# Gate, second half: the block sums of pair 10 are given the room of two kept activation sums of down and are fetched right behind the pair's raw tile

## The chip, the cores and the metric

The kernel runs on one core of a Trainium2 chip. What is compared is the time on the device in microseconds (us) for one launch: three runs of the kernel before took 1110.24, 1110.93 and 1111.15 us, and their median, 1110.93 us, stands for it. Beside the runs there is one profiled execution, whose trace names every instruction of the five engines: PE (matrix products; its weight loads are listed apart as PEld), DVE (vector), ACT (scalar), POOL and SP. SP computes nothing here; it issues the DMA transfers one behind the other, and if one has to wait, all behind it wait too. Times inside the execution are counted from the start of its span.

## What is computed

One encoder layer over 256 tokens of width 2048 in float32: a mixer (SSD heads beside pooling heads), a gated conv-MLP, and last a gate for an embedding that belongs to the layer. The change sits in the last of these:

```python
ff = conv_glu(hn, w_ffn_up[i], ffn_conv_w[i], ffn_conv_b[i], w_ffn_down[i])   # ends with "down": 5632 -> 2048
h = h + rmsnorm(ff, ffn_norm_post[i])
gate = jax.nn.sigmoid(rmsnorm(h, ple_norm_pre[i]) @ w_ple_gate[i])            # "gate": 2048 -> 2048
h = h + rmsnorm(gate * (p[i] @ w_ple[i]), ple_norm_post[i])
```

## The kernel before

The stages follow each other: input projection, mixer, output projection, up, down (names that begin with dn), the embedding product (ple) and gate (names that begin with gt). Every large product is made on PE. A weight is split in two parts that PE takes, a rounded one (h, an ACT cast, line 153) and the rest (l, a DVE subtraction, line 154), and each product of two blocks is three matmuls: high by high, low by high, high by low.

Down and gate make their 2048 output columns in two halves of 1024. Each half runs over the input rows in **pairs** of 128-row tiles. A pair is worked in one of two ways:

- plainly: one raw tile of weights (128x2048, 1 MB) is fetched, split in two casts and two subtractions, and gives 24 matmuls of 512 columns;
- with seven products (`seven_products`): the pair and the two groups of 128 tokens make a 2x2 by 2x2 block product, which is done with seven block products instead of eight, on sums of blocks: 21 matmuls. The weights' side of it needs three raw blocks (tile `r`, 128x1536, 768 KB) and four sums of blocks (tile `t`, 128x2048, 1 MB). The split parts are a and b (of r) and d and c (of t). The sums of most pairs were made in the idle time of up and stored in device memory; then `t` is fetched like `r`.

In the second half of gate the pairs come in the order 0, 8, 10, 12, 2, 4, 6, 14 (each named by its first tile), and 8, 10 and 12 are worked with seven products: tiles gt18r, gt18t, gt110r, gt110t, gt112r and gt112t. Behind the last of them, and behind the matmuls of pair 2 (casts gth, rests gtl, raw gt1r), DVE folds the seven products into the four accumulators (`combine`, lines 310 to 324); the matmuls of pair 4 that add to an accumulator come only when its fold is done. Three raw tiles follow pair 12: those of pairs 4, 6 and 14.

**Rooms.** Raw tiles share three rooms, casts and rests five each, and everything of 128x2048 that comes and goes (pages) shares 13 rooms. A tile gets a room when the last reader of the tile before it in that room is done. A fetch is therefore held until its room is free. `seven_products` asks for `t` as a page. In down, three of the activations' sums (k = 8, 18, 24, the list `OWN`) are made once in the first half and kept for the second, each in a room of its own of 128x1024 (`own_place`).

**Order.** In this part of the program no order is written out by hand: a scheduler places the instructions of each engine by when it thinks their operands and rooms are there. A fetch through `load` may be placed freely (`ahead`) or is tied behind the fetch before it (`last["dma"]`); only names that begin with dn1 (`IN_ORDER`) are tied.

Of the kernel before, what the change touches and what calls it, by code (L numbers as in the profile page):

```python
# [11 lines left out]
F32 = mybir.dt.float32  # L12
F32R = mybir.dt.float32r
# [4 lines left out]
P = 128  # L18
# [35 lines left out]
def build(nc, a, out):  # L54
# [6 lines left out]
    with tile.TileContext(nc) as tc, \  # L61
# [9 lines left out]
        def ins(r):  # L71
            return getattr(r, "ins", r)

        def page(name, dtype=F32):
            return gp.tile([P, 2048], dtype, tag="pg", bufs=13, name=name)
# [13 lines left out]
        def mm(o, lhsT, rhs, start, stop):  # L89
            last["pe"] = ins(nc.tensor.matmul(o, lhsT, rhs, start=start, stop=stop, skip_group_check=True))  # L90
# [24 lines left out]
        last, sums_ = {}, {}  # L115

        def load(dst, src, ahead=False):

            with tc.issue_after(last["dma"]) if last and not ahead else nullcontext():
                return ins(nc.sync.dma_start(dst, src))  # L120
# [21 lines left out]
        def split(name, src, nel, cuts=()):  # L142

            if name in ready:
                return ready.pop(name)
            if name in spare:
                hi, lo = spare.pop(name)
            else:
                hi = wp.tile([P, 1056], F32R, tag="whi", bufs=5, name=f"{name}h")
                lo = wp.tile([P, 1056], F32R, tag="wlo", bufs=5, name=f"{name}l")  # L150
            for c0, c1 in zip((0, *cuts), (*cuts, nel)):
                s = slice(c0, c1)
                last["act"] = ins(nc.scalar.copy(hi[:, s], src[:, s]))
                last["dve"] = ins(nc.vector.tensor_sub(lo[:, s], src[:, s], hi[:, s].bitcast(F32)))
            return hi, lo

        def raw(name, src=None):
            r = wp.tile([P, 2048], F32, tag="raw", bufs=3, name=name)
            if src is not None:
                last["dma"] = load(r, src, not name.startswith(IN_ORDER))  # L160
            return r
# [33 lines left out]
        IN_ORDER = ('dn1',)  # L195
# [70 lines left out]
        def add_blocks(r, t=None):  # L266

            v = r.rearrange("p (b c) -> p b c", b=4)
            s = v if t is None else t.rearrange("p (b c) -> p b c", b=4)
            for i, a, b in ((1, v, 0), (0, v, 3), (3, s, 1), (2, s, 3)):  # L270
                nc.vector.tensor_add(s[:, i], v[:, i], a[:, b])  # L271

        def seven_products(name, stage, w, k0, c0, a_, acc, alt, start, stop):

            if (stage, c0, k0) in sums_:
                r = raw(f"{name}r")
                last["dma"] = load(r[:, 512:], w[c0 // 1024, k0 // 2][:, 512:], not name.startswith(IN_ORDER))
                t, held = sums_[stage, c0, k0]  # L280
                if not held:
                    t = page(f"{name}t")
                    last["dma"] = load(t, sums_[stage, c0, k0][0], not name.startswith(IN_ORDER))
            else:
                r = t = raw(f"{name}r", w[c0 // 1024, k0 // 2])
                if stage in APART:
                    t = page(f"{name}t")
                    add_blocks(r, t)
            b11 = split(f"{name}a", r[:, 512:1024], 512)
            b2 = split(f"{name}b", r[:, 1024:], 1024)  # L290
            if r is t:
                add_blocks(r)
            t42 = split(f"{name}d", t[:, 1024:], 1024)
            t31 = split(f"{name}c", t[:, :1024], 1024)

            for x, (wh, wl), c, o, own in (
                    ("a11", b11, 0, alt[0], True), ("a12", b2, 0, acc[0][0], False), ("a22", t42, 0, acc[1][0], False),
                    ("s4", b2, 512, acc[0][1], False), ("s2", t42, 512, alt[3], True), ("s1", t31, 512, alt[1], True),
                    ("s3", t31, 0, alt[2], True)):
                xh, xl = a_[x]  # L300
                for q, (xx, ww) in enumerate(((xh, wh), (xh, wl), (xl, wh))):
                    mm(o, xx, ww[:, c:c + 512], own and start and q == 0, own and stop and q == 2)
# [23 lines left out]
        def token_major(name, w, c0, ks, get, acc, tail=1, fast=(), alt=None, sums=None, at=()):  # L326
# [3 lines left out]
            for u in range(nu):  # L330
# [3 lines left out]
                if u in fast:  # L334
                    if u == fast[0]:
                        alt = alt + [misc(f"{name}s{i}") for i in (2, 3)]
                    seven_products(f"{name}{k0}", name[:2], w, k0, c0, sums(k0), acc, alt, u == fast[0], u == fast[-1])
                    continue
# [143 lines left out]
        for u in range(0, NK, 2):  # L482
            r = [wp.tile([P, 2048], F32, tag="raw", bufs=3, name=f"dtur{u}") if u else r0, page(f"dtur{u + 1}")]
            for j in range(2):
                k = u + j
# [17 lines left out]
            for j in range(2):  # L503
                k = u + j
# [412 lines left out]
        lp = early.enter_context(tc.tile_pool(name="late", bufs=1))  # L917
# [49 lines left out]
        for i, w_ in enumerate(which[2:] + which[:2]):  # L967
            fetch, add, store = block_sums(*w_, i >= len(which) - 2)
            n = 45 * i // 10 + 4
# [135 lines left out]
        own, own_pages = {}, []  # L1105

        def own_place(k):
            n = OWN.index(k)
            if n < 3:
                return lp.tile([P, 1024], F32R, name=f"hd{k}")  # L1110
            if n % 2 == 1:
                own_pages.append(page(f"hd{k}", F32R))
            return own_pages[-1][:, (n - 1) % 2 * 1024:((n - 1) % 2 + 1) * 1024]

        def hid_sums(k):

            (h2, l2), (h1, l1) = get_hid(k, 3 * P), get_hid(k + 1)
            if k in own:
                d = own[k]
            else:  # L1120
                o = own_place(k) if k in OWN else mid(f"hd{k}", F32R)
                if k in kept:
                    nc.gpsimd.dma_start(o.bitcast(F32), kept[k])
                    d = sums_in(o)
                else:
                    d = hid_sums_of(k, sp.tile([P, 512], F32, tag="junk", bufs=1, name=f"hs{k}"), o)
                if k in OWN:
                    own[k] = d
            return dict(d, a11=(h1[:, :P], l1[:, :P]), a12=(h2[:, :P], l2[:, :P]), a22=(h2[:, P:], l2[:, P:]))
# [198 lines left out]
```

## Time and profile before

| | |
|---|---|
| median of three runs | 1110.93 us |
| profiled execution, its own time | 1110.88 us |
| its span | 1109.1 us |
| PE busy | 1099.8 us (99% of the span) |
| DVE busy | 972.4 us (88%) |
| ACT busy | 728.4 us (66%) |
| granted clock of PE, mean | 0.998 |
| transferred over the DMA engines | 362.24 MB, mean 327 GB/s |

Lines of the trace give the start in us, the duration in us, the engine, the line of the kernel and the operation, then the tile written and the tiles read, without buffer numbers (gt110t is one tile; `gt` stands for any of the accumulators of gate), sizes, and the count of merged instructions (x2). In brackets stands how long the engine had been idle before and what ended it. A matmul of 512 columns is listed with some 0.39 us, and in a run without gaps the next begins 0.23 us after it: they overlap, so a late matmul is seen by the distance of two starts.

### The profile page before, as it was taken

The numbers are of one execution on the slowest core, as the hardware profiler recorded it, in microseconds if no ns is written. First come the engines' busy times: TensorE is split into PE (matmuls) and PEld (weight loads), VectorE is DVE, ScalarE is ACT, GpSimd is POOL, SyncE is SP. The second block draws the span as 40 slices with busy tenths as digits, with TensorE's granted clock in tenths as the row PEclk, the third lists the DMA queues.
The fourth block names the chain that finished last, engine by engine and source line by source line (L and its number), as shares of the span: only waits on it lengthen the run. The fifth ranks groups of instructions, "written<-read, shape, count | busy, mean of one in ns | idle before, by whom it ended". The sixth has DMA issues, their size and how long they took to land.

```text
span 1109.1 us, 16105 instructions
## 1 busy us (share of the span) xinstructions
PE 1099.8 (99%) x5949; PEld 948.4 (86%) x5949; DVE 972.4 (88%) x1359; ACT 728.4 (66%) x1065; POOL 74.3 (7%) x146
## 2 busy tenths in 40 slices
PE   9999999999999999999999999999999999999997
PEld 9999988888888888888888888888888888888876
DVE  6589997898879898888888888988999998999996
ACT  7958763556775565655655646657678777877673
POOL 0200000100100000000000000000000000001001
PEclk9999999999999999999999999999999999999999
DMA  9985358556499999999999998999999889996772
GB/s 364 363 334 190 111 192 343 209 217 230 181 358 400 400 399 356 379 362 361 394 358 381 360 388 345 402 358 422 381 393 375 352 332 384 419 388 242 270 294 76
DMA packets 57247, 362.24 MB, mean 327 GB/s; under 512 B 6352, under 2 KB 7248, under 8 KB 21200
## 3 DMA queue, kind: packets, MB, share of 16 engines
q1 hardware_dynamic: 45504, 298.71, 68.9%
q0 software_dynamic: 11232, 61.87, 14.6%
q8 instruction: 47, 0.77, 0.3%
q10 hardware_dynamic: 432, 0.62, 0.2%
q14 instruction: 32, 0.26, 0.1%
HBM read 307.18 MB, written 54.00 MB: 326 GB/s over the span
## 4 chain that ended last, share of the span: by engine, by line
PE 95%; DVE 2%; ACT 1%; issue 1%; DMA 1%; POOL 0%; POOLq 0%; ACTq 0%
PE ga L90 22%; PE va L90 22%; PE dna L90 11%; PE woa L90 6%; PE xbc L90 5%; PE dns L90 4%; PE dtu L90 4%; PE z L90 4%; PE gt L90 4%; PE dn0s L90 2%; PE dn1s L90 2%; PE ple L90 1%; DMA gt112t<-gts 1%; PE yd L90 1%; PE wos L90 1%
## 5 line engine op out<-in xcount | busy, mean ns | idle before, releaser
L90 PE MATMUL ga<-wox,ug_0h 128*128 128x512 f32 x352 | 125.5, 395 | 0.0
L90 PE MATMUL ga<-wox,ug_1h 128*128 128x512 f32 x352 | 125.2, 394 | 0.0
L90 PE MATMUL va<-wox,uv_0h 128*128 128x512 f32 x352 | 124.8, 393 | 0.0
L90 PE MATMUL va<-wox,uv_1h 128*128 128x512 f32 x352 | 124.8, 393 | 0.0
L90 PE MATMUL ga<-wox,ug_1l 128*128 128x256 f32 x352 | 99.1, 282 | 0.0
L90 PE MATMUL va<-wox,uv_0l 128*128 128x256 f32 x352 | 99.1, 281 | 0.0
L90 PE MATMUL va<-wox,uv_1l 128*128 128x256 f32 x352 | 99.1, 281 | 0.0
L90 PE MATMUL ga<-wox,ug_0l 128*128 128x256 f32 x352 | 99.0, 281 | 0.0
L271 DVE TENSOR_TENSOR dnb<-dnb 128x512 f32<-128x512 f32 x128 | 88.3, 690 | 3.0
L90 PEld LDWEIGHTS va<-wox,uv_0h 128*128 128x128 f32 x352 | 66.1, 188 | 15.0
L90 PEld LDWEIGHTS ga<-wox,ug_1h 128*128 128x128 f32 x352 | 66.1, 188 | 15.0
L90 PEld LDWEIGHTS va<-wox,uv_1h 128*128 128x128 f32 x352 | 66.1, 188 | 15.0
L90 PEld LDWEIGHTS ga<-wox,ug_0h 128*128 128x128 f32 x352 | 66.1, 188 | 14.8
L90 PEld LDWEIGHTS ga<-wox,ug_0l 128*128 128x128 f32 x352 | 66.2, 188 | 0.1
L90 PEld LDWEIGHTS ga<-wox,ug_1l 128*128 128x128 f32 x352 | 66.2, 188 | 0.0
L90 PEld LDWEIGHTS va<-wox,uv_1l 128*128 128x128 f32 x352 | 66.2, 188 | 0.0
L90 PEld LDWEIGHTS va<-wox,uv_0l 128*128 128x128 f32 x352 | 66.2, 188 | 0.0
L246 POOL DMA_DIRECT2D dns<-dnb x30 | 16.1, 536 | 320.9 <-DVE dnb L271 280.5
L839 ACT CAST he<-he 128x512 fp32r<-128x512 f32 x13 | 8.1, 620 | 41.1 <-DVE he L838 41.1
L981 ACT CAST hs<-hid 128x384 fp32r<-128x384 f32 (+1 forms) x44 | 23.4, 539 | 16.6 <-PE dna L90 16.3
L1041 ACT ACTIVATE fc<-gr,vt 128x256 f32<-128x256 f32 x44 | 26.1, 594 | 5.9 <-DVE gr L1034 5.9
L398 ACT COPY hid<-va 128x256 f32<-128x256 f32 x44 | 15.6, 372 | 19.5 <-PE va L90 19.5
(2452 smaller groups left out, 3275.5 us busy)
## 6 DMA issues: line engine op xcount, KB each, us to landing
dnb<-w_down SPq DMA_DIRECT2D x32, 1024.0 KB, 9.9
dns<-dnb POOLq DMA_DIRECT2D x30, 1024.0 KB, 5.9
hd<-hsum POOLq DMA_DIRECT2D x25, 512.0 KB, 8.1
zr<-w_z SPq DMA_DIRECT2D x8, 1024.0 KB, 4.8
dtur<-w_dtu SPq DMA_DIRECT2D x14, 528.0 KB, 8.8
hsum<-he POOLq DMA_DIRECT2D x13, 512.0 KB, 8.1
wo0r<-w_out_ SPq DMA_DIRECT2D x6, 1024.0 KB, 7.0
gtb<-w_gate SPq DMA_DIRECT2D x6, 1024.0 KB, 9.5
```

Source lines behind the costliest of these rows:

```text
L90: last["pe"] = ins(nc.tensor.matmul(o, lhsT, rhs, start=start, stop=stop, skip_group_check=True))
L246: nc.gpsimd.dma_start(t, pg[0])
L271: nc.vector.tensor_add(s[:, i], v[:, i], a[:, b])
L398: nc.scalar.copy(o[:, f * L:(f + 1) * L], acc[f][:, L:])
L839: nc.scalar.copy(o[:, :512], s[:, :512])
L981: nc.scalar.copy(t[:, :c1], hid_part(k)[:, :c1])
L1041: nc.scalar.activation(c[:, f], v[:, f], AF.Identity, bias=vec(V_FCB + 4 * s + 2 * i + f), scale=vec(w + NF))
```

## The change

```diff
                 if not held:
-                    t = page(f"{name}t")
-                    last["dma"] = load(t, sums_[stage, c0, k0][0], not name.startswith(IN_ORDER))
+                    t = lp.tile([P, 2048], F32, tag="own", bufs=1, name=f"{name}t") if name == "gt110" else page(f"{name}t")
+                    last["dma"] = load(t, sums_[stage, c0, k0][0], not name.startswith((*IN_ORDER, "gt110")))
...
             if n < 3:
-                return lp.tile([P, 1024], F32R, name=f"hd{k}")
+                if n == 2:
+                    return lp.tile([P, 1024], F32R, name=f"hd{k}")
+                if n == 0:
+                    own_pages.append(lp.tile([P, 2048], F32R, tag="own", bufs=1, name="hd"))
+                return own_pages[0][:, n * 1024:(n + 1) * 1024]
```

The kept sums of k = 8 and k = 18 of down now lie side by side in one room of 128x2048, tagged "own"; that of k = 24 stays as it was. The memory taken is the same. When gate comes to pair 10 of its second half, its tile gt110t takes this room instead of a page, and its fetch is tied behind that of gt110r. Nothing is computed differently, and the number of computing instructions and of fetches on every engine is the same. Up to the issue of gt110r the built program is the same instruction by instruction, waits included (apart from names); from there to the end some rows move.

**The fetches.** SP, around gt110r (fetches of gate's second half; gts is the stored sums in device memory). Before:

```order
L120 DMA gt18r<-w_gate 128x1536
L120 DMA gt110r<-w_gate 128x1536
L120 DMA gt112r<-w_gate 128x1536
L120 DMA gt18t<-gts_8_7212 128x2048
L120 DMA gt110t<-gts_10_7342 128x2048
L120 DMA gt1r_10453<-w_gate 128x2048
L120 DMA gt112t<-gts_12_7461 128x2048
```

and now:

```order
L120 DMA gt18r<-w_gate 128x1536
L120 DMA gt110r<-w_gate 128x1536
L120 DMA gt110t<-gts_10_7342 128x2048
L120 DMA gt112r<-w_gate 128x1536
L120 DMA gt18t<-gts_8_7212 128x2048
L120 DMA gt112t<-gts_12_7461 128x2048
L120 DMA gt1r_10452<-w_gate 128x2048
```

gt110t moved ahead of gt112r and gt18t. The page that gt110t had goes to gt112t, which takes gt110t's old place behind gt18t and waits for that page's last reader, as gt110t did (the last DVE operation of line 1236 in the first half); before, gt112t had the page of gt18t and waited for DVE's gt18cl.

**The splits of pair 12.** DVE, from the last raw part of pair 12 (gt112bl) to the folds of `combine`. Before:

```order
L154 TENSOR_TENSOR gt112bl<-gt112r,gt112bh 128x1024
L154 TENSOR_TENSOR gtl_10291<-gt1r_10453,gth_10290 128x1024 x2
L154 TENSOR_TENSOR gt112dl<-gt112t,gt112dh 128x1024
L154 TENSOR_TENSOR gt112cl<-gt112t,gt112ch 128x1024
L312 TENSOR_TENSOR gt1v_10471<-gt1v_10471,gt1s_10329 128x512
L314 TENSOR_TENSOR gt1v_10472<-gts_1_10289,gt1v_10471 128x512
L316 TENSOR_TENSOR gt1v_10472<-gt1s_10328,gt1v_10471 128x512
L313 TENSOR_TENSOR gt_0_10284<-gt_0_10284,gt1v_10471 128x512
L317 TENSOR_TENSOR gt_0_10286<-gt_0_10286,gt1v_10472 128x512
L315 TENSOR_TENSOR gt_1_10285<-gt_1_10285,gt1v_10472 128x512
L154 TENSOR_TENSOR gtl_10293<-gt1r_10487,gth_10292 128x1024
```

and now:

```order
L154 TENSOR_TENSOR gt112bl<-gt112r,gt112bh 128x1024
L154 TENSOR_TENSOR gt112dl<-gt112t,gt112dh 128x1024
L154 TENSOR_TENSOR gt112cl<-gt112t,gt112ch 128x1024
L154 TENSOR_TENSOR gtl_10290<-gt1r_10452,gth_10289 128x1024 x2
L312 TENSOR_TENSOR gt1v_10470<-gt1v_10470,gt1s_10328 128x512
L154 TENSOR_TENSOR gtl_10292<-gt1r_10486,gth_10291 128x1024
L313 TENSOR_TENSOR gt_0_10283<-gt_0_10283,gt1v_10470 128x512
L314 TENSOR_TENSOR gt1v_10471<-gts_1_10288,gt1v_10470 128x512
L316 TENSOR_TENSOR gt1v_10471<-gt1s_10327,gt1v_10470 128x512
L315 TENSOR_TENSOR gt_1_10284<-gt_1_10284,gt1v_10471 128x512
L317 TENSOR_TENSOR gt_0_10285<-gt_0_10285,gt1v_10471 128x512
```

The two subtractions of pair 12's sums moved ahead of the two of pair 2, and the first of pair 4 (gtl_10292) moved in between the first fold and the others. On ACT the two casts of pair 12's sums moved from behind both casts of pair 2 to between them.

**The matmuls behind pair 12.** PE's rows 5696 to 5702 on either side, counted from the start of PE's list, with what they wait for (gt_0_10286 and gt_0_10285 are the same accumulator, that of the second token group; gt_0_10284 and gt_0_10283, and gt_1_10285 and gt_1_10284, are those of the first). Before:

```order
L90 MATMUL gt_1_10285<-gth_10290,dnxl_9795 128x512
L90 MATMUL gt_0_10284<-gth_10292,dnxh_9793 128x512 [waits DVE_49,Activation_49]
L90 MATMUL gt_0_10286<-gth_10290,dnxh_9793 128x512 [waits DVE_49]
L90 MATMUL gt_0_10286<-gtl_10291,dnxh_9793 128x512
L90 MATMUL gt_0_10286<-gth_10290,dnxl_9795 128x512
L90 MATMUL gt_1_10285<-gth_10292,dnxh_9793 128x512 [waits DVE_49]
L90 MATMUL gt_0_10286<-gth_10290,dnxh_9793 128x512
```

and now:

```order
L90 MATMUL gt_1_10284<-gth_10289,dnxl_9794 128x512
L90 MATMUL gt_0_10283<-gth_10291,dnxh_9792 128x512 [waits DVE_49,Activation_49]
L90 MATMUL gt_0_10283<-gtl_10292,dnxh_9792 128x512
L90 MATMUL gt_0_10283<-gth_10291,dnxl_9794 128x512
L90 MATMUL gt_0_10283<-gth_10291,dnxh_9792 128x512 [waits Activation_49]
L90 MATMUL gt_1_10284<-gth_10291,dnxh_9792 128x512 [waits DVE_49]
L90 MATMUL gt_1_10284<-gtl_10292,dnxh_9792 128x512
```

The first row that waits for a fold (5697, the fold of line 313) stands where it stood; the second is row 5701 now (line 315) where it was row 5698 (line 317). Before this place, rows 5670 to 5684, the 15 matmuls of pair 12 that remain run now in one piece, in the order dh, dl, dh, ..., where before they were interleaved with matmuls of pair 2. Behind it, the last matmul that adds to the first accumulator is row 5737 instead of 5739, and that of the second 5741 instead of 5743. The first narrow matmul (256 columns) is row 5757 on both sides. On ACT, in the output of the second token group, the square of its first 512 columns (line 1243) moved ahead of the tanh (line 1234) of the next 256.

## The prediction

> **What bounds the kernel now.** I read the page's busy times first, then PE's waits, then the timeline around the one wait in gate, then the chain of waits and SP's list.
>
> ```profile
> span 1109.1 us, 16105 instructions
> PE 1099.8 (99%) x5949; PEld 948.4 (86%) x5949; DVE 972.4 (88%) x1359; ACT 728.4 (66%) x1065; POOL 74.3 (7%) x146
> ```
>
> PE is busy for all but 9.3 us, so little but PE's gaps can be gained. Among its waits in the whole program this one lies in the stretch of the change:
>
> ```profile
> PE gt L90 <- ACT gt112dh L153: 0.7, 1, 0.7
> ```
>
> PE's timeline there (of the runs between, only the ends are shown):
>
> ```profile
> 1071.53 0.39 PE L90 MATMUL gts<-gt112ah,dnxh 128*128 128x512 f32 x1
> ...
> 1072.91 0.39 PE L90 MATMUL gt<-gt112bh,psp 128*128 128x512 f32 x1
> 1073.99 0.50 PE L90 MATMUL gt<-gt112dh,dnxh 128*128 128x512 f32 x1 [0.69 <-ACT gt112dh L153]
> 1074.32 0.40 PE L90 MATMUL gt<-gt112bl,psp 128*128 128x512 f32 x1
> ...
> 1079.87 0.40 PE L90 MATMUL gt<-gth,dnxl 128*128 128x512 f32 x1
> 1080.20 1.00 PE L90 MATMUL gt<-gth,dnxh 128*128 128x512 f32 x2
> 1081.04 0.40 PE L90 MATMUL gt<-gtl,dnxh 128*128 128x512 f32 x1
> ...
> 1094.35 0.28 PE L90 MATMUL gt<-gth,dnxh 128*128 128x256 f32 x1
> ```
>
> From 1071.53 to 1072.91 are 6 steps, 0.23 us each. From 1071.53 (row 5664 of PE's list) to 1094.35 (row 5757) are 93 steps, which would take 21.39; they took 22.82. So **1.43 us** are lost here. They are 1.08 - 0.23 = 0.85 at gt112dh, 0.10 on the next step, 0.10 before 1080.20, and 0.84 - 2 x 0.23 = 0.38 before 1081.04. The first two (0.95) come from the late tile gt112t, the last two (0.48) from PE waiting for DVE's folds of `combine`. What is late, by the chain of waits:
>
> ```profile
> 1065.74 7.07 DMA gt112t<-gts
> ```
>
> and why, by SP's timeline:
>
> ```profile
> 1049.53 0.33 SPq L120 DMA_DIRECT2D gt110r<-w_gate  x1
> 1054.52 0.33 SPq L120 DMA_DIRECT2D gt112r<-w_gate  x1
> 1054.94 0.39 SPq L120 DMA_DIRECT2D gt18t<-gts  x1
> 1059.92 0.33 SPq L120 DMA_DIRECT2D gt110t<-gts  x1
> ...
> 1067.48 7.03 SPq L120 DMA_DIRECT2D gt1r<-w_gate  x3
> ```
>
> gt112t could not be issued before DVE had done with gt18t, whose page it takes. It landed 7.07 later, at 1072.81, and its cast began at once.
>
> **The change part by part.** The fetches first, with the times to landing:
>
> ```profile
> gt18t<-gts SPq DMA_DIRECT2D x1, 1024.0 KB, 6.7
> gt110t<-gts SPq DMA_DIRECT2D x1, 1024.0 KB, 5.9
> ...
> gt110r<-w_gate SPq DMA_DIRECT2D x1, 768.0 KB, 4.1
> gt112r<-w_gate SPq DMA_DIRECT2D x1, 768.0 KB, 4.4
> ```
>
> gt110t is issued right behind gt110r, at about 1049.9. Its room was last read in the second half of down, far back, so it adds no wait; SP then holds gt112r until 1054.52 as before, so issuing one more fetch (0.4) costs nothing. gt110r lands at 1053.63. What a further 1 MB behind a transfer costs is seen at gt18t: 1061.64 against 1058.92 for gt112r just ahead of it, 2.72. So gt110t lands near 1056.35. gt112r landed at 1058.92 and needs 0.75 x 2.72 = 2.04 for its bytes, so its stretch begins at 1056.88: gt110t just fits in front, and gt18t is not later. gt112t goes to gt110t's old place, 1059.92, with the same neighbours, and lands by gt110t's row at 1065.8, 7 us earlier than now.
>
> The splits next, ACT and then DVE:
>
> ```profile
> 1061.72 1.05 ACT L153 CAST gt18dh<-gt18t 128x1024 fp32r<-128x1024 f32 x1 [1.03 <-DMA gt18t<-gts]
> ...
> 1065.96 1.05 ACT L153 CAST gt110dh<-gt110t 128x1024 fp32r<-128x1024 f32 x1 [0.77 <-DMA gt110t<-gts]
> ...
> 1068.39 1.05 ACT L153 CAST gt112bh<-gt112r 128x1024 fp32r<-128x1024 f32 x1
> 1069.75 2.00 ACT L153 CAST gth<-gt1r 128x1024 fp32r<-128x1024 f32 x2 [0.32 <-DVE gt110cl L154]
> ```
>
> ```profile
> 1063.36 1.22 DVE L154 TENSOR_TENSOR gt18dl<-gt18t,gt18dh 128x1024 fp32r<-128x1024 f32 x1
> ...
> 1070.24 1.22 DVE L154 TENSOR_TENSOR gt112bl<-gt112r,gt112bh 128x1024 fp32r<-128x1024 f32 x1
> 1071.78 2.36 DVE L154 TENSOR_TENSOR gtl<-gt1r,gth 128x1024 fp32r<-128x1024 f32 x2 [0.33 <-ACT gth L153]
> 1074.06 1.22 DVE L154 TENSOR_TENSOR gt112dl<-gt112t,gt112dh 128x1024 fp32r<-128x1024 f32 x1
> ...
> 1079.37 0.69 DVE L313 TENSOR_TENSOR gt<-gt,gt1v 128x512 f32<-128x512 f32 x1
> ...
> 1080.56 0.69 DVE L315 TENSOR_TENSOR gt<-gt,gt1v 128x512 f32<-128x512 f32 x1
> ```
>
> ACT's 0.77 before gt110dh goes, but it is worth nothing by itself: DVE has no gap there,
>
> ```profile
> 1059.90:1065.70 5.80, 5.80 (x27) 4.46 (x25) 5.80 (x8) 4.26 (x8) 1.18 (x1) 1.00 0.76 307
> ```
>
> (PE, PEld, then DVE 5.80 of 5.80; the 1.00 is the granted clock) and runs on to 1071.46. Then it counts. Two subtractions of 1024 columns take 2.36, so one slot is 1.14, and one of 512 columns 0.60 (1079.37 to 1080.56 are two). ACT now casts the first half of pair 2 (raw landed, see below, at 1068.6), then gt112dh, whose room is free once PE has read gt110bh for the last time:
>
> ```profile
> 1069.22 0.40 PE L90 MATMUL gt<-gt110bh,psp 128*128 128x512 f32 x1
> ```
>
> that is at 1069.62. So gt112dh is cast from about 1069.7 to 1070.7, gt112ch to 1071.7. DVE does gt112dl from 1071.4 and gt112cl to 1073.7, pair 2's two rests (gtl) to 1076.0. PE needs gt112dh at 1072.91 (its matmul is row 5670 now, where gt112bh was), gt112dl at 1073.14 (done 1072.6), gt112cl at 1075.21 (done 1073.7), pair 2's rests at 1076.59 and 1077.28 (done 1074.9 and 1076.0). Every cover is 0.5 us or more: **the 0.95 at pair 12 goes**.
>
> The folds come next, and they take something back. PE reaches row 5697 at 1079.12 without a gap. DVE's list by then: first fold (line 312) 1075.9, the first rest of pair 4 1076.55 to 1077.8, the fold of line 313 at 1077.95 (when PE has ended row 5690, 1077.9) to 1078.64, then lines 314, 316 and 315 in slots of 0.60; line 315 ends at 1080.44. Row 5697 waits for line 313: free. Row 5701 waits for line 315: PE is there at 1080.04 and goes on at 1080.50, **0.46 lost** where 0.48 were lost before. Bounds for this place: nothing (line 315 one slot earlier) and 1.6 (one more slot of 1.14 ahead of it). Behind it the rests of pairs 4, 6 and 14 end at 1082.8 to 1088.0, each 0.2 to 0.6 ahead of its first matmul.
>
> Sum on PE: 0.95 + 0.48 - 0.46 = 0.97. The tail must follow:
>
> ```profile
> 1095.25 2.75 DVE L1205 SCALAR_TENSOR_TENSOR vg<-vg,go0r,hb 128x512 f32<-128x512 f32 x4 [1.15 <-POOL go0r L409]
> ...
> 1098.63 0.63 ACT L1243 ACTIVATE gth<-gth 128x512 f32<-128x512 f32 x1 [0.70 <-DVE gth L1236]
> ...
> 1100.30 0.47 ACT L1234 ACTIVATE gth<-gts,rh 128x256 f32<-128x256 f32 x1
> ...
> 1100.73 0.55 POOL L1187 TENSOR_TENSOR gth<-go1m,half_up 128x1 f32<-128x1 f32 x1
> ```
>
> Two arms meet there within 0.1: PE's last matmul, whose tanh begins at 1100.30 (0.97 earlier now), and the squares that POOL sums (1100.73). The second starts from the first accumulators, 2 rows = 0.46 earlier in PE's list, thus 1.43 earlier; but ACT now does the square (0.63 and its read-out) ahead of the tanh of 256 columns (0.47), which gives back about 0.5. Both arms: **0.9 us**. Span 1109.1 - 0.9 = 1108.2; the profiled execution's own time, 1110.88, lies 0.05 under the median of the runs, so the median goes from 1110.93 to **1110.0 us** (-0.08%).
>
> **The rivals.** *The folds eat the gain.* DVE now has pair 4's first rest ahead of the fold of line 313, so a late raw tile holds the folds. The raws of pairs 2 and 4 took
>
> ```profile
> gt1r<-w_gate SPq DMA_DIRECT2D x1, 1024.0 KB, 7.5
> ...
> gt1r<-w_gate SPq DMA_DIRECT2D x1, 1024.0 KB, 8.1
> ```
>
> from 1061.10 and 1067.48: landed 1068.6 and 1075.6. The cast of the second then ends at 1076.65, just as DVE wants it (1076.55). Each us later costs one at row 5701; 0.9 late makes it nothing: 1110.9. Against it: gt112t's 1 MB is no longer in front of this raw.
>
> *Slower: gt18t comes late behind gt110t.* The calculation above had 0.5 us to spare. If gt110t moves at half speed (another 2.7), gt18t lands 2.2 late, ACT casts gt18dh at 1063.9 and DVE begins gt18dl at 1065.05 instead of 1063.36, 1.7 late, and as DVE has no gap, all behind it and PE are 1.7 late: 1110.0 + 1.7 = 1111.7. It costs from 0.6 late on and turns the sign from 1.5 late on. For it: at 1061.72 ACT already waited 1.03 for this very tile. Against it, the stretch into which gt110t moves, with the DMA engines' busy share, 0.44, next to last:
>
> ```profile
> 1049.50:1054.50 5.00, 5.00 (x24) 4.05 (x23) 4.76 (x8) 2.44 (x4) 0.00 (x0) 1.00 0.44 159
> ```
>
> The Trainium skill, "DMA: Bandwidth & Descriptors" (Queues, rings and completion order), speaks for this rival: on each DMA engine the descriptors of one queue are taken in ring order, so gt110t stands whole in front of gt112r and gt18t. By that rule the delay is what gt110t has left at 1056.88, by the rows above nothing.
>
> *All 1.43 go*, because the folds come a slot earlier than I count: 1109.4. For it, only that no cover is needed; against it, DVE's full list.
>
> *It does not do what it says*, the room not being free at 1049.9: SP would hold gt112r too. The lists show waits that ended long before, so I give it nothing.
>
> **How the numbers follow.** My forecast 0.65 (its own range 1109.6 to 1110.5); folds 0.15; late gt18t 0.10; all gaps 0.10. The three runs before spread by 0.9, so each case carries 0.45 either way; the range is 1109.1 (all gaps, with some of the spread) to 1111.4 (most of the slower case). About 0.2%, which is 2.2 us, is what a measurement of this kernel can tell from no change; PE's gaps in this stretch are 1.43 in all, so faster by more needs something not in the profile: 0.06. Slower by more needs gt18t over 3.7 late: 0.04. Within: 0.90.
>
> **What would show it.** Right: gt110t issued near 1049.9, gt112t near 1059.9 and landed by 1066; no PE gap at gt112dh; a gap of about half a us at a matmul that waits for line 315; the first narrow matmul at 1093.4. Wrong: ACT waiting more than 1.6 for gt18t, or PE gaps between 1078 and 1082 that sum to over 1 us.

## The result, and the profile after

| | before | after |
|---|---|---|
| median of 22 runs each, us | 1110.62 | 1112.10 |
| lowest to highest, us | 1109.39 to 1112.01 | 1110.83 to 1115.46 |
| ratio of the runs, with its 95% interval | | 1.0015 (1.0008 to 1.0022) |
| the profiled execution's own time, us | 1110.88 | 1111.36 |
| its span, us | 1109.1 | 1109.5 |

The kernel became slower by about 1.5 us, where 0.9 us less was forecast. The whole interval lies above 1, and the median lies outside the predicted range, by 0.7.

The page after, busy times:

```profile
span 1109.5 us, 16103 instructions
PE 1099.9 (99%) x5949; PEld 948.2 (85%) x5949; DVE 972.9 (88%) x1359; ACT 728.1 (66%) x1065; POOL 74.8 (7%) x146
```

They say nothing: PE does the same work. Its waits after the change (total us, times, longest) do; three more, none of them in this stretch, are as before:

```profile
PE gt L90 <- ACT gt18dh L153: 1.2, 1, 1.2
PE gt L90 <- DVE gt L315: 0.3, 1, 0.3
PE gts L90 <- ACT gt18ch L153: 0.2, 1, 0.2
```

The wait for gt112dh (0.7 before) is gone, and a longer one for gt18dh has come, 10 us earlier in the program, together with one for the fold of line 315. In this execution everything ahead of 1049 ran 0.54 earlier than in the one of before (the first matmul of gt18ah begins at 1061.05, before at 1061.59), so I compare distances. PE's timeline after:

```profile
1061.05 0.39 PE L90 MATMUL gts<-gt18ah,dnxh 128*128 128x512 f32 x1
...
1062.89 0.39 PE L90 MATMUL gt<-gt18bh,psp 128*128 128x512 f32 x1
1064.47 0.50 PE L90 MATMUL gt<-gt18dh,dnxh 128*128 128x512 f32 x1 [1.19 <-ACT gt18dh L153]
1064.81 0.40 PE L90 MATMUL gt1s<-gt18dh,psp 128*128 128x512 f32 x1
1065.42 0.50 PE L90 MATMUL gts<-gt18ch,psp 128*128 128x512 f32 x1 [0.21 <-ACT gt18ch L153]
...
1073.83 0.39 PE L90 MATMUL gt<-gt112bh,dnxl 128*128 128x512 f32 x1
1074.06 0.40 PE L90 MATMUL gt<-gt112dh,dnxh 128*128 128x512 f32 x1
...
1080.99 0.39 PE L90 MATMUL gt<-gth,dnxh 128*128 128x512 f32 x1
1081.68 0.50 PE L90 MATMUL gt<-gth,dnxh 128*128 128x512 f32 x1 [0.30 <-DVE gt L315]
```

With 0.23 as the step of a run without gaps, 1.58 - 0.23 = 1.35 are lost at gt18dh and 0.61 - 0.23 = 0.38 at gt18ch, none at gt112dh, and 0.69 - 0.23 = 0.46 at line 315. What feeds gt18dh, on ACT and then DVE:

```profile
1063.37 1.04 ACT L153 CAST gt18dh<-gt18t 128x1024 fp32r<-128x1024 f32 x1 [3.23 <-DMA gt18t<-gts]
```

```profile
1064.45 1.23 DVE L154 TENSOR_TENSOR gt18dl<-gt18t,gt18dh 128x1024 fp32r<-128x1024 f32 x1 [1.55 <-ACT gt18dh L153]
```

ACT stood for 3.23 before it got gt18t (1.03 before), and DVE, which had no gap here, for 1.55. The transfers, from SP's timeline and from the list of DMA issues with their time to landing (KB, then us):

```profile
1048.99 0.33 SPq L120 DMA_DIRECT2D gt110r<-w_gate  x1
1049.42 0.37 SPq L120 DMA_DIRECT2D gt110t<-gts  x1
1053.98 0.33 SPq L120 DMA_DIRECT2D gt112r<-w_gate  x1
1054.36 0.42 SPq L120 DMA_DIRECT2D gt18t<-gts  x1
1059.38 0.33 SPq L120 DMA_DIRECT2D gt112t<-gts  x1
```

```profile
gt110t<-gts SPq DMA_DIRECT2D x1, 1024.0 KB, 6.6
gt18t<-gts SPq DMA_DIRECT2D x1, 1024.0 KB, 8.9
gt112t<-gts SPq DMA_DIRECT2D x1, 1024.0 KB, 7.1
...
gt112r<-w_gate SPq DMA_DIRECT2D x1, 768.0 KB, 6.5
```

gt110t landed at 1056.0, within 0.2 of the prediction (1056.35, less the 0.54 by which this execution is earlier). But gt112r took 6.5 (4.4 before) and gt18t 8.9 (6.7 before), although gt110t was out of the way. Between them part of the DMA engines paused. By stretches of 1 us (the last two numbers are the busy share of the DMA engines and GB/s), before and then after:

```profile
1055.00:1056.00 1.00, 1.00 (x6) 0.83 (x5) 1.00 (x3) 0.80 (x2) 0.00 (x0) 1.00 0.31 104
1056.00:1057.00 1.00, 1.00 (x6) 0.79 (x6) 1.00 (x3) 0.90 (x2) 0.00 (x0) 1.00 1.01 313
```

```profile
1054.00:1055.00 1.00, 1.00 (x6) 0.83 (x5) 1.00 (x2) 0.34 (x1) 0.00 (x0) 1.00 1.11 436
1055.00:1056.00 1.00, 1.00 (x6) 0.79 (x5) 1.00 (x3) 1.00 (x2) 0.00 (x0) 1.00 0.56 209
1056.00:1057.00 1.00, 1.00 (x6) 0.83 (x5) 1.00 (x3) 0.90 (x3) 0.00 (x0) 1.00 0.69 240
```

A kernel that has three fetches queued here, one behind the other, runs its DMA engines at 0.56 and 0.69 for two microseconds. Each of these fetches leaves 16 signals in the trace, as many as there are DMA engines; I take each to be one engine's. In the kernel before, gt112r's 16 signals come within 0.7 us; after, 8 of them come at 1057.6 to 1057.8 and the other 8 at 1059.1 to 1060.5, and gt18t's spread likewise over 3.2.

The packets in the trace tell a late start from a slow transfer (gt112r's are the only ones of 6144 bytes at this place). On either side its first packet began about 0.95 us after the issue, at 1055.48 before and 1054.94 after, and at first at most eight ran at a time. Before, sixteen ran at a time 0.8 later, from 1056.25 on. After, still only eight ran until 1056.25, and sixteen packets were under way again only from 1057.5 on. The median packet took no longer (0.25 us, before 0.28). So about half of the engines took up gt112r late, and gt18t, behind it on the same engines, inherits this.

The Trainium skill, "DMA: Bandwidth & Descriptors" (Queues, rings and completion order), states that each engine takes a queue's descriptors in ring order. The trace agrees: gt110t, gt112r and gt18t land in that order, at 1056.0, 1060.5 and 1063.3; the order alone does not make the second follow the first at once.

### The profile page after: what moved, and what is told of

It is laid out like the page before. It is cut to its first block, busy times and chain, and to the rows that moved or that the text cites. A ratio compares the mean times of both kernels' runs of the same rounds, so it can differ in the third digit from the quotient of the medians.

```text
span 1109.5 us, 16103 instructions
## 1 busy us (share of the span) xinstructions
PE 1099.9 (99%) x5949; PEld 948.2 (85%) x5949; DVE 972.9 (88%) x1359; ACT 728.1 (66%) x1065; POOL 74.8 (7%) x146
## 4 chain that ended last, share of the span: by engine, by line
PE 96%; ACT 1%; DVE 1%; DMA 1%; issue 1%; POOL 0%; POOLq 0%; SPq 0%; ACTq 0%
PE ga L90 22%; PE va L90 22%; PE dna L90 11%; PE woa L90 6%; PE xbc L90 5%; PE dns L90 4%; PE dtu L90 4%; PE z L90 4%; PE gt L90 4%; PE dn0s L90 2%; PE dn1s L90 2%; PE ple L90 1%; DMA gt18t<-gts 1%; PE gts L90 1%; PE yd L90 1%; PE wos L90 1%
```

## The experiments

**The theories.** A: the fetch of gt110t in front of gt112r and gt18t makes gt18t late, and all else follows from that. B: the new order of the splits at pair 12, of the folds and of the tail costs the time. C: the clock that PE is granted. D: the joined room of the kept sums in down. The times of the kernel before differ between groups of runs, since each group was compared with it on its own chip.

**The change again,** unchanged, with a second profile.

> The changed kernel once more, for a second profile. Theory A (gt110t, set in front of gt112r and gt18t, makes gt18t late): gt18t lands 8 to 10 us after its issue (6.7 before), PE loses 1 to 2 us at the matmuls of pair 8 that wait for gt18dh and gt18ch, nothing at gt112dh, and 0.4 to 0.6 at line 315; 1111.5 to 1112.7 in the median. Theory B (the new order of ACT, DVE and PE at pair 12 and in the tail costs the time): gt18t may be late or not, and the time lost lies between 1074 and the end. Theory C (the clock granted at the end): the two matmuls into gof take 1.5 us or more, as in the first profile (1.79 against 1.13 before), and the loss is there; by A they may be short again, around 1.1.

Measured: 1112.01 against 1110.37, ratio 1.0017 (1.0009 to 1.0026). gt18t took 9.4, and PE lost 1.87 at gt18dh, 0.38 at gt18ch (2.25, a little over what A said), 0 at gt112dh and 0.47 at line 315. The matmuls into gof were short again: the copy that follows them waits 1.22, as before, and not 1.88 as in the first profile of the change, where they are

```profile
1103.32 1.79 PE L90 MATMUL gof<-vg,godg 128*128 128x512 f32 x2 [1.92 <-ACT godg L1200]
```

against 1.13 for this pair in the first profile of before. The granted clock fell to 0.50 at 1103.64, in the middle of these last two matmuls, and that cost 0.66. The stretch ahead of the fall:

```profile
1100.23:1103.64 3.41, 1.50 (x6) 0.64 (x5) 1.91 (x5) 1.75 (x6) 1.36 (x3) 1.00 0.02 4
```

All 14 profiles have such a fall near their end, between 1103.1 and 1110.0; in ten it comes behind the last matmul and costs nothing, and of the other four only two are of the change (0.66 and, in its third profile, 0.12; gt112r behind gt18t has 0.35 and half a fetch more 0.52, both further down). So A holds, and C in this form is chance: it depends on where the fall comes.

But this execution, 1116.13 long, shows something else. PE's time and granted clock (the number before the last two) in four stretches of 3.41 us around the pause:

```profile
1062.18:1065.59 3.41, 3.41 (x17) 2.77 (x16) 3.41 (x6) 0.86 (x4) 1.25 (x1) 1.00 0.96 326
1065.59:1069.01 3.42, 1.50 (x6) 0.64 (x5) 1.35 (x3) 2.23 (x3) 0.00 (x0) 1.00 0.99 412
1069.01:1072.42 3.41, 3.41 (x9) 2.64 (x9) 3.41 (x5) 2.96 (x4) 0.00 (x0) 0.50 0.19 79
1072.42:1075.83 3.41, 3.41 (x17) 2.76 (x16) 3.40 (x4) 2.84 (x5) 0.00 (x0) 1.00 0.69 269
```

Behind a stretch in which PE was busy for only 1.50 of 3.42, the clock is 0.50 for the next 3.41: 9 matmuls where 17 fit, 8/17 of 3.41 = 1.6 lost on top of the gap. The rest of the 1116.13 was lost elsewhere (1.5 of it at a wait of PE for ACT's hs in down, which the two other profiles of the change don't have).

**gt110t behind gt18t, in its own room.**

```diff
-                    last["dma"] = load(t, ..., not name.startswith((*IN_ORDER, "gt110")))
+                    with tc.issue_after(last["gt18t"]) if name == "gt110" else nullcontext():
+                        last["dma"] = load(t, ..., not name.startswith(IN_ORDER))
+                    last[f"{name}t"] = last["dma"]
```

> gt110t keeps the room of its own, but its fetch is tied behind that of gt18t, so SP's order is gt110r, gt112r, gt18t, gt110t, gt112t. Theory A: gt18t lands 6.5 to 7.2 us after its issue again, no PE gap at gt18dh, gt112t is still fetched about 5 us before the time it had in the kernel before and the gap at gt112dh stays away; 0.5 to 1.0 us under the kernel before: 1109.6 to 1110.2. Theory B: the order of the splits at pair 12 is that of the change, so it is as slow as the change, 1111.5 to 1112.7. Theory C: as B, with gof matmuls of 1.5 or more. Theory D (the joined room of the kept sums costs time in down): as slow as the change, with the loss ahead of 1040.

Measured: 1110.06 against 1110.37, 0.9997 (0.9989 to 1.0006).

```profile
gt18t<-gts SPq DMA_DIRECT2D x1, 1024.0 KB, 6.6
```

gt112t was issued at 1059.57, nothing lost at gt18dh or gt112dh, 0.46 at the fold of line 315. All of the change but the place of one fetch is in this kernel, and the loss is gone. The medians are 0.3 apart where A said 0.5 to 1.0, and the kernel is not shown to be faster than the one before.

**gt110t behind gt18r,** one place earlier than in the change.

```diff
-                last["dma"] = load(r[:, 512:], ...)
+                last["dma"] = last[f"{name}r"] = load(r[:, 512:], ...)
...
-                    last["dma"] = load(t, ..., not name.startswith((*IN_ORDER, "gt110")))
+                    with tc.issue_after(last["gt18r"]) if name == "gt110" else nullcontext():
+                        last["dma"] = load(t, ..., not name.startswith(IN_ORDER))
```

> gt110t in its own room, fetched one place earlier: tied behind gt18r, ahead of gt110r, near 1045. Theory A: gt110r then lands 2 to 3 us later than it did, for which its cast near 1058 has cover; the queue is empty again before gt112r, so gt18t lands 6.5 to 7.2 after its issue, no gap at gt18dh and none at gt112dh: 0.5 to 1.0 us under the kernel before, 1109.6 to 1110.2. Theories B, C and D: 1111.5 to 1112.7.

Measured: 1110.06 against 1110.37, 0.9996 (0.9987 to 1.0004). Its DMA issues and PE's only remaining wait in gate:

```profile
gt110t<-gts SPq DMA_DIRECT2D x1, 1024.0 KB, 6.4
gt18t<-gts SPq DMA_DIRECT2D x1, 1024.0 KB, 6.8
gt112t<-gts SPq DMA_DIRECT2D x1, 1024.0 KB, 5.8
...
gt110r<-w_gate SPq DMA_DIRECT2D x1, 768.0 KB, 4.6
gt112r<-w_gate SPq DMA_DIRECT2D x1, 768.0 KB, 4.4
```

```profile
PE gt L90 <- DVE gt L316: 0.3, 1, 0.3
```

(Line 316 there is line 315 of the change.) gt112r and gt18t are as quick as before, since nothing is in flight when they are issued. Here too the medians are 0.3 apart and not 0.5 to 1.0. These two kernels have the splits, the rooms and the tail of the change: B and D fall.

**One fetch more in the kernel before:** its rooms for gt110t and gt112t and its order, and in the joined room (its edit is that of the change) 1 MB that nothing reads, behind gt110r.

```diff
+                if name == "gt110":
+                    load(lp.tile([P, 2048], F32, tag="own", bufs=1, name="gtx"), sums_[stage, c0, k0][0])
                 t, held = sums_[stage, c0, k0]
```

> The kernel before (gt110t and gt112t in pages, its order of fetches and splits) with the joined room, and one fetch more: 1 MB of pair 10's stored sums into the joined room, which nothing reads, behind gt110r where the change has gt110t. Theory A: gt18t lands 8 to 10 us after its issue, PE loses 1 to 2 us at gt18dh and gt18ch, and gt112t comes later too since its page is that of gt18t, so 0.7 or more stays lost at gt112dh: 1112 to 1114, slower than the kernel before by 1.5 or more. Theories B and C: nothing is moved on ACT, DVE and PE, so 1110.3 to 1111, no difference.

Measured: 1112.37 against 1110.37, 1.0017 (1.0008 to 1.0026). The issue list and PE's waits:

```profile
gtx<-gts SPq DMA_DIRECT2D x1, 1024.0 KB, 6.9
gt18t<-gts SPq DMA_DIRECT2D x1, 1024.0 KB, 9.3
...
gt112r<-w_gate SPq DMA_DIRECT2D x1, 768.0 KB, 6.9
```

```profile
PE gt L90 <- ACT gt18dh L153: 1.6, 1, 1.6
```

A fetch that nothing reads costs as much as the change. My expectation had one miss: 0.7 or more was to stay lost at gt112dh, and only 0.11 did, since PE itself came 2 us later there.

**The joined room alone** (gt110t a page, the order of the kernel before), against the changed kernel:

```diff
-                    t = lp.tile([P, 2048], F32, tag="own", ...) if name == "gt110" else page(f"{name}t")
-                    last["dma"] = load(t, ..., not name.startswith((*IN_ORDER, "gt110")))
+                    t = page(f"{name}t")
+                    last["dma"] = load(t, ..., not name.startswith(IN_ORDER))
```

> Only the joined room of the kept sums of k = 8 and 18 in down; gt110t stays a page and SP's order is that of the kernel before. Theory A (a fetch in front of gt112r and gt18t makes gt18t late) and theories B and C: as the kernel before, 1110.0 to 1110.9, gt18t 6.5 to 7.2 us from issue to landing, the gap of about 0.7 idle at gt112dh. Theory D (the joined room itself costs time): slower by 0.5 or more, with the loss ahead of 1040.

Measured: 1110.40 against 1110.63, 1.0002 (0.9993 to 1.0011): no cost in the median, as A, B and C expected. But the gap at gt112dh was 0.31 here (0.95 in the profile of before), with gt112t landing 6.4 after its issue instead of 7.1. I come back to this. Two of its 11 runs took 1112.62 and 1113.55, without a profile.

**gt112r behind gt18t:** the changed kernel with SP's order gt110r, gt110t, gt18t, gt112r.

```diff
-                last["dma"] = load(r[:, 512:], w[c0 // 1024, k0 // 2][:, 512:], not name.startswith(IN_ORDER))
+                with tc.issue_after(last["gt18t"]) if name == "gt112" else nullcontext():
+                    last["dma"] = load(r[:, 512:], w[c0 // 1024, k0 // 2][:, 512:], not name.startswith(IN_ORDER))
...
+                    last[f"{name}t"] = last["dma"]
```

> The changed kernel with gt112r tied behind gt18t, so SP's order is gt110r, gt110t, gt18t, gt112r, gt112t. Theory A: gt18t, now the first to be issued while gt110t is in flight, is the one whose slower half of the DMA engines starts late; in the changed kernel that half took up gt112r at about 1057.2, so gt18t lands by 1060.5 (6.0 to 6.8 us after its issue), 1 us ahead of the kernel before, and there is no gap at gt18dh; gt112r lands near 1063, far ahead of its cast: 1109.5 to 1110.2. Theory B: as slow as the change, 1111.5 to 1112.7.

Measured: 1110.01 against 1110.63, 0.9996 (0.9987 to 1.0005); nothing lost at gt18dh and gt112dh. (The profile is of the slowest of its 11 runs, 1112.33; PE waits 1.3 in it for hs in down, as in the second profile of the change, and the clock falls in the last two matmuls.) The way there was another than I expected. SP's timeline:

```profile
1051.71 0.33 SPq L120 DMA_DIRECT2D gt110r<-w_gate  x1
1052.14 0.37 SPq L120 DMA_DIRECT2D gt110t<-gts  x1
1052.61 0.38 SPq L120 DMA_DIRECT2D gt18t<-gts  x1
1056.70 0.33 SPq L120 DMA_DIRECT2D gt112r<-w_gate  x1
```

gt18t needs no wait of its own: it was issued 0.47 behind gt110t, and was issued late in the other kernels only because it stood behind gt112r, which waits 4 us for its room. It landed at 1061.86, PE's first matmul of gt18ah being at 1063.77, so 1.9 ahead of PE, where it landed 0.05 behind in the kernel before. And no pause is seen, sixteen packets being under way at a time from 1057 to 1062: gt112r, issued 5.2 ahead of gt18t's landing, landed 1.9 behind it, in the changed kernel, issued 2.0 ahead of gt110t's landing, 4.5 behind it.

**Half a fetch more** in the kernel before (512 KB, read by nothing), against the kernel with one fetch more:

```diff
-                    load(lp.tile([P, 2048], F32, tag="own", bufs=1, name="gtx"), sums_[stage, c0, k0][0])
+                    load(lp.tile([P, 2048], F32, tag="own", bufs=1, name="gtx")[:, :1024], sums_[stage, c0, k0][0][:, :1024])
```

> As the kernel with one fetch more, which nothing reads, but of half the size (512 KB). Version 1 of theory A (what counts is that gt112r is issued while another fetch is still in flight): the half fetch lands 0.3 to 1 us behind the issue of gt112r, so part of the DMA engines start gt112r late, gt18t takes 7.5 to 9.5 us, and 0.5 to 1.5 us are lost at gt18dh: 1111 to 1112.3. Version 2 (what counts is the bytes in front): 0.5 MB less is in front, and it has gone through before gt112r's stretch, so gt18t takes 6.5 to 7.2 us and the time is that of the kernel before, 1110.0 to 1110.9.

Measured: 1110.38 against 1110.63, 0.9995 (0.9986 to 1.0004). gt112r took 4.4 and gt18t 6.6. Version 2 came out. Version 1 is too coarse: the extra fetch was still in flight when gt112r was issued (its last signal came 1.4 later), but by the packets' times in the trace its data had stopped moving before gt112r's began (the last of its packets ended 0.93 behind the issue of gt112r, whose first began 0.96 behind it).

**Three quarters of a fetch more** (768 KB, `:1536` in both places).

> As the kernel with one fetch more, of three quarters of its size (768 KB). With 512 KB nothing was lost (its packets ended 0.3 us behind the issue of gt112r), with 1 MB gt18t was 2.5 late (they ended 1.7 behind it). If what counts is that packets still run when gt112r is taken up, 1.2 us behind its issue, this one is near the edge: its packets end about 1.0 behind the issue, gt18t takes 6.5 to 7.8 us, and 0 to 0.6 is lost at gt18dh: 1110.0 to 1111.2. If the delay grows with the bytes, half the delay of 1 MB: gt18t takes about 8, 0.5 to 0.9 lost, 1110.9 to 1111.6.

Measured: 1111.02 against 1110.59, 1.0004 (0.9994 to 1.0014), so unclear in the time; in the profile gt112r took 5.8, gt18t 8.1, and PE lost 0.55 at gt18dh and 0.38 at gt18ch. That is the size that I gave for a delay that grows with the bytes. With half a fetch showing no delay at all, it reads more as an edge between 0.5 and 1 MB than as a proportion; one profile of each size does not show which. (The 0.3 and 1.7 in the expectation should be 0.93, as said above, and 1.9.)

**gt18t surely late:** the 1 MB that nothing reads is fetched twice, before and behind gt112r.

```diff
+                if name == "gt110":
+                    gtx = lp.tile([P, 2048], F32, tag="own", bufs=1, name="gtx")
+                    for _ in range(2):
+                        last["dma"] = load(gtx, sums_[stage, c0, k0][0])
                 t, held = sums_[stage, c0, k0]
```

> As the kernel with one fetch more (1 MB, read by nothing), and the same 1 MB fetched once again between gt112r and gt18t, so that gt18t is surely late. Theory A: gt18t lands 2.5 to 5 us later than with one extra fetch, near 1067, and PE stands for 3.5 to 5 us ahead of gt18dh. Theory C in the form that the second profile of the change suggests (a pause of PE that fills most of one 3.41 us stretch has the clock granted at 0.5 for the next 3.41 us, which costs 1.7): one stretch of about 3.41 us at 0.5 follows the pause, and the time is 1115 to 1117; without that effect the clock stays 1.00 until the tail, and the time is 1113.3 to 1115.

Measured: 1115.50 (5 runs) against 1110.63, 1.0044 (1.0032 to 1.0057). PE's wait, and the same four stretches around it:

```profile
PE gt L90 <- ACT gt18dh L153: 3.2, 1, 3.2
```

```profile
1062.15:1065.56 3.41, 1.86 (x9) 1.18 (x7) 1.50 (x3) 0.00 (x0) 0.00 (x0) 1.00 1.01 428
1065.56:1068.97 3.41, 1.50 (x5) 0.97 (x6) 1.74 (x2) 2.81 (x4) 0.00 (x0) 1.00 1.01 428
1068.97:1072.39 3.42, 3.42 (x9) 2.64 (x8) 3.42 (x5) 2.61 (x3) 0.00 (x0) 0.50 0.75 249
1072.39:1075.80 3.41, 3.41 (x16) 2.78 (x15) 3.04 (x4) 3.18 (x4) 0.00 (x0) 1.00 1.01 413
```

gt18t landed at 1066.1, 1.4 later than with one extra fetch where A said 2.5 to 5, PE lost 3.40 at gt18dh by the distance of its starts, just under A's 3.5 to 5, and the clock was 0.50 for one stretch, as the second form of C said. In the two profiles that have it, the pause cost itself and 1.6 more.

**The kernel before twice, the change once more,** each one execution with a profile, to see how much of the first profiles was chance.

> The kernel before, unchanged, for a second profile of it. Two kernels with its order of fetches (the joined room alone, and the half fetch) showed only 0.31 and 0.24 lost at gt112dh, where the first profile showed 0.95. If the first profile was a late sample: gt112t lands 5 to 6.6 us after its issue here and 0 to 0.5 is lost at gt112dh. If the gap is steady: gt112t takes about 7 and 0.8 to 1.0 is lost.

> The kernel before once more, a third profile of it, with the same two expectations: 0 to 0.5 lost at gt112dh if the first profile was a late sample, 0.8 to 1.0 if the gap is steady.

> The changed kernel, a third profile of it. Theory A: gt18t lands 8 to 10 us after its issue, 1.2 to 2.2 lost at gt18dh, and nothing at gt112dh. Theory C (a pause of PE of some 2 us that falls into one 3.41 us stretch has the clock at 0.5 for the next 3.41 us): the clock dips only if more than about 2 us of such a stretch are idle; with a loss of under 1.8 it stays at 1.00 until the tail.

Measured, with the others (us lost by PE, from the distances of its starts; single steps of 0.1 are left out at pair 8 and, where the splits are those of the change, at the folds; the last column runs from the first matmul of gt18ah to the copy of gof, the last work of ACT):

| profile | gt18t landed after | lost at pair 8 | gt112t landed after | lost at gt112dh | lost at the folds | to the end |
|---|---|---|---|---|---|---|
| before, first | 6.7 | 0 | 7.1 | 0.95 | 0.5 | 42.5 |
| before, second | 6.7 | 0 | 7.4 | 1.24 | 0.5 | 42.8 |
| before, third | 6.6 | 0 | 6.3 | 0.23 | 0.5 | 41.8 |
| joined room alone | 6.7 | 0 | 6.4 | 0.31 | 0.5 | 41.9 |
| change, first | 8.9 | 1.7 | 7.1 | 0 | 0.5 | 44.1 (0.7 the clock) |
| change, second | 9.4 | 2.3 | 6.9 | 0 | 0.5 | 45.5 (1.6 the clock) |
| change, third | 8.6 | 1.4 | 7.0 | 0 | 0.5 | 43.1 (0.1 the clock) |
| gt110t behind gt18t | 6.6 | 0 | 6.6 | 0 | 0.5 | 41.7 |
| gt110t behind gt18r | 6.8 | 0 | 5.8 | 0 | 0.5 | 41.7 |

Neither of my two expectations for the kernel before came out alone: the gap at gt112dh was larger in the second profile and nearly gone in the third. It hangs on when gt112t lands. In the third profile of the change the clock stayed at 1.00 until the tail, with 0.99 (A said 1.2 to 2.2) and 0.38 lost at pair 8. The last column gives, in the middle of three, 42.5 before and 44.1 after, +1.6. That this is the shift of the medians of the runs (1.5 and 1.6) is partly luck: without what the clock cost, the three of the change are 43.4, 43.9 and 43.0, which is +0.9. Two of the three profiles of before have a large gap at gt112dh; against gt110t behind gt18r, which has none and was measured on the same chip as the second profile of the change, it is +1.8 (43.44 and 41.67), and the medians are 1.95 apart (1112.01 and 1110.06). So the late gt18t is the largest part of the loss, and three profiles of each do not settle how much of the 1.5 is the clock's.

## Why the prediction was wrong

**Where it failed: the first step,** "gt110t just fits in front, and gt18t is not later". Its first half was right: issued at 1049.42, landed at 1056.0 (predicted 1056.35, which is 1055.81 with the earlier start). Then I took 2.72 per MB as the price of one fetch behind another, from gt18t behind gt112r, and let gt112r's stretch begin when gt110t ended. That pair was issued 0.4 apart, 4.0 ahead of gt112r's landing. gt112r was now issued 2.0 ahead of gt110t's landing, and followed it 4.5 later instead of 2.04. That stretch was also too short already in the trace of before: gt112r's data moved there from 1055.48 on, not from 1056.88, so that the 0.5 to spare did not exist. The row that carries this price was already among my own: gt110t of the kernel before, issued at 1059.92, took 5.9 and landed at 1065.86; gt18t ahead of it had landed at 1061.64. So it came 4.2 behind a fetch ahead of whose landing it had been issued 1.7. I read that row as a landing time and not as the price of a fetch that is issued shortly before the queue runs empty. With it: 1056.0 + 4.2 + 2.8 = 1063.0 for gt18t, and 1063.3 was measured (that it comes so near is in part luck, since the row is of 1 MB and gt112r is of 0.75). The sign that I had named for being wrong came: ACT waited 3.23 for gt18t, over 1.6.

The trace of before has this for the whole program. Worked out from the issues and landings of SP's 1 MB fetches, with leads over 6 left out; "lead" is the time from its issue to the last signal of the fetch ahead on SP, of whatever size, "follows" the median time from that signal (or from its own issue, if later) to its own landing; the last column holds the middle 80% of the fetches:

```
lead, us       before alone: count, follows      all 14 profiles: count, follows, 10% to 90%
queue empty       26   4.9                          359   4.9   4.7 to 6.8
0 to 1            12   6.1                          178   5.9   4.1 to 7.4
1 to 2            15   5.1                          202   5.1   3.1 to 6.2
2 to 3            11   4.0                          160   3.8   2.5 to 5.1
3 to 4            16   2.8                          237   2.7   2.5 to 4.3
4 to 5            32   2.8                          422   2.6   2.5 to 4.0
5 to 6            28   2.8                          386   2.6   2.5 to 4.0
```

In these traces a fetch issued 3 us or more ahead of the end of the one in front follows it, in the median, at 2.6 to 2.8 per MB. With less lead it pays up to all of its own start. With a lead of 1 to 2 it comes even later than an empty queue would have brought it: 4.9 from its issue is 2.9 to 3.9 behind the one in front, and it comes 5.1 behind.

**The empty queue was an asset.** I quoted the DMA engines' share of 0.44 in the stretch ahead as evidence against a late gt18t. It was the reverse: because the queue was empty, gt112r had sixteen packets under way within 0.8 us of its first, and gt18t right behind it. Filling the empty stretch took that away.

**The other steps.** *gt112t is issued 6 us earlier:* right (1059.38). It landed 7.1 after and not 5.9, which no one waited for. *The gap at gt112dh goes:* right in all three profiles of the change; but its size was that of one execution. Over the three profiles of before it is 0.95, 1.24 and 0.23. *The folds give back 0.46 at row 5701, behind line 315:* right, 0.46 and 0.47 in every kernel with these splits; another 0.11 is lost on the step behind it, which the sum did not have. *The tail follows with 0.9:* right where gt18t is in time: with gt110t behind gt18r, PE's first matmul of gt18ah to the last operand of gof (godg) is 40.06, in the first profile of before 40.91, 0.85 less; against the third, in which the gap was 0.23, it is 0.12 less. So the sum as such stands for a kernel in which the fetch has another place and against an execution with that large a gap; and the runs of those kernels, with medians 0.3 to 0.6 below and intervals that reach past 1, cannot tell it from no change. *2.2 us is what a measurement can tell:* too coarse, with 22 runs each the interval of the ratio is 1.5 us wide, and it lies wholly above 1.

**The rivals.** The slower one, "gt18t comes late behind gt110t", is what happened: 2.2 late, as priced there, and 1111.7 against 1112.1. I gave it 0.10. Its cause was not the one it names: gt110t was not slow, gt112r was taken up late. That its 2.2 came out is luck, since they stand on a halved speed of gt110t that no run shows. The 1.7 that it prices are what PE lost at pair 8 in the first profile; the two others have 2.3 and 1.4. It also lacked a term. Of the 35 runs of the change, 8 took over 1113.1, of 97 of the kernel before none; the one of these 8 with a profile has the half clock behind the pause at gt18dh (and 1.5 lost in down), and the kernel with gt18t surely late shows the same stretch of half clock. That it is the cause in the other seven was not shown, and the joined room alone, without that pause, had one run of 11 at 1113.55. A wait of PE for hs in down of over a microsecond (1.5 and 1.3) is in 2 of the 11 profiles of kernels with the joined room and in none of the 3 of before; whether the room has a part in it no run shows.

The Trainium skill, "TensorE: Matmul & The Clock Gate" (Part 1: The HAM clock gate), states that the array falls to half its clock after an idle window of some 3.4 us that runs freely. The length agrees with the 3.41 here; idle the stretch need not be: 1.50 of 3.42 busy sufficed twice, 1.86 did not (first of the four stretches of the kernel with gt18t surely late), nor did 2.02 in the first profile of the change:

```profile
1062.67:1066.09 3.42, 2.02 (x8) 1.06 (x7) 1.87 (x3) 2.72 (x4) 0.00 (x0) 1.00 0.98 414
1066.09:1069.50 3.41, 3.41 (x17) 2.73 (x16) 3.41 (x4) 3.41 (x5) 0.00 (x0) 1.00 0.16 65
```

The tails bear this out. Cut into stretches of 3.413 us from the first change of the clock in the trace, each of the 14 profiles has its clock fall near the end behind a stretch in which PE was busy for 1.12 to 1.53, and in no profile did it fall behind one of 1.86 or more.

**What stays open:** why it is about half of the DMA engines that take up the next fetch late, and what they wait for; no run looked into that. Also open are what made the longest runs so long, those without a profile, and how the 1.5 divides between the late tile and the clock.

## What to carry to other kernels

Before a fetch is moved into an idle stretch of its queue, look at who is issued next, and how long before the moved one ends: in these traces a follower with less than about 3 us of lead pays much of its start again, on the engines that take it up last, and what counts for the waiting operation is the last of the 16 signals. A price for "one transfer behind another" holds only for the lead at which it was measured. A gap seen in one profile is one sample: before it is put into a sum as a gain, look at how the landing that ends it varies.

## What I had not expected of the hardware

- A 768 KB fetch issued 2.0 ahead of the landing of the one in front landed 4.5 behind it, with half of its signals 1.5 to 2.9 behind the first; issued 5.2 ahead of another, 1.9 behind it.
- The edge is narrow, by one profile each: with the extra fetch's landing 1.4, 1.6 and 2.0 behind the issue of gt112r (512, 768 and 1024 KB; the last in the kernel with gt18t surely late), gt112r took 4.4, 5.8 and 6.0; with 1.9 to 2.1 in the three profiles of the change 6.4 to 7.0.
- PE at half clock for 3.41 us behind a stretch in which it had still been busy for 1.50 of 3.42. In the 14 profiles the edge lies between 1.53 and 1.86 busy.
